# A 192-byte pad tile ahead of the FFN pool: four moving operands at another SBUF offset

## The chip, the cores and the metric

The kernel runs on one core of one Trainium2 chip. The metric is the device time of one execution in microseconds (us); the median of three executions of the kernel before is 2823.21 us.

## The reference

A decoder block on one sequence of 256 positions with 2048 channels, in float32. Two token mixers run on the same normalised input, their results are gated and merged, and a dense gated feed-forward network (FFN) follows. What matters for this change is the FFN:

```
def swiglu(h, w_gate_up, w_down):
    gate, up = jnp.split(h @ w_gate_up, 2, axis=-1)
    return (jax.nn.silu(gate) * up) @ w_down
...
x = x + gate_m[:, None, :] * mix                        # the mixers' half, ending with a projection w_o
h = modulate(rms_norm(x, norm_ffn_w[layer]), shift_f, scale_f)
x = x + gate_f[:, None, :] * swiglu(h, w_gate_up[layer], w_down[layer])
return rms_norm(x, final_norm_w)
```

The hidden width of the FFN is 5632, 44 tiles of 128.

## The kernel before

**Tiling.** Activations lie transposed: 128 channels on the partitions, 256 positions along the free dimension. A weight block is 128 x 1024 floats (512 KB): eight 128 x 128 tiles. Every weight of the block is read once, in such blocks.

**A block's way.** `load_next` (L131 to L147) issues the block's DMA into a ring of five `raw` tiles, ScalarE rounds it to `hi` (L144, type float32r), VectorE subtracts to get `lo` (L146). Up to four blocks are taken in ahead. For each 128 x 128 tile TensorE then runs three matmuls (L214 to L216 in `lin_items`; L237 to L239, the same, in `quad_items`; L1111 to L1113 for the last of the state-space mixer):

```
T_.matmul(ps[:, t, :], hi[:, s], h_, start=kt == 0, stop=False)
T_.matmul(ps[:, t, :], hi[:, s], al[:, kt, :], start=False, stop=False)
T_.matmul(ps[:, t, :], lo[:, s], h_, start=False, stop=kt == nk - 1)
```

The weights `hi`, `lo` are the stationary operand (one LDWEIGHTS each); the activations are the moving operand, 128 x 256, likewise split in a high and a low part. 24 such matmuls make a block. Below, three in a row, high-high, high-low, low-high, are called a triple.

**Order.** The code fixes every engine's order (`tc.manual_schedule()`); `pump()` emits one block's matmuls, then a step of the running mixer, then work on finished products. There is no planner. Stages in order of time: the adaLN scales and first products, eight units of the delta-rule mixer, eight of the state-space mixer, the merge, the projection `w_o` (32 blocks), the FFN's `w_gu` (176 blocks: 12 by `quad_items`, 164 by `lin_items`), the FFN's `w_dn` (88 blocks), the final norm.

**Where the moving operands lie.** Tiles of a pool follow one another in SBUF, and a pool opens where the last open one ends. The addresses of the built program, in bytes of each partition:

| tile | pool | used in | first byte | remainder by 512 |
|---|---|---|---|---|
| `hh`, `hl` | ap | both mixers' input products | 106176, 122560 | 192 |
| `yh`, `yl` | gl | mixers' output products | 169664 to 181952 | 192 |
| `mh`, `ml` | gl, mp | `w_o` | 138944, 147136, 186048 | 192 |
| `h2h`, `h2l` | ff | `w_gu` | 82432, 98816 | 0 |
| `fh`, `fl` | ff | `w_dn` | 115200, 160256 | 0 |
| `hi`, `lo` (stationary) | wp | everywhere | 66048, 29184 and on in steps of 4096 | 0 |

A moving slice is 1024 bytes long and a stationary one 512, so the remainder is that of every slice. The `ff` pool opens (L1174) after the mixers' pools are closed and so begins where `ca`, a pool of the mixers' constants, had begun. Its tiles in order: `h2h`, `h2l`, `fh`, `fl` (L1175 to L1178), the rotating `fth`/`htmp`, and `gf`, `sq`, `rstd`, which VectorE and ScalarE alone use. Before the first FFN matmul, L1184 to L1187 build `h2h` and `h2l`, sixteen steps of VectorE, ScalarE, VectorE.

Of the kernel before, what the change touches and what calls it, by code (L numbers as in the profile page):

```python
# [10 lines left out]
F32 = mybir.dt.float32  # L11
# [8 lines left out]
P = 128  # L20
# [5 lines left out]
NG = 8  # L26
FT = 44
BLK = 8
# LA: weight blocks kept ready ahead of the matmuls; NRAW, NAR: rings of raw blocks and of ada rows
LA = 3  # L30
NRAW = 5
# blocks between two halves of ada rows, by phase
SIDE, SIDE2 = 2, 8
SIDE3 = 6
# gate pairs of the ssm branch that fill the first gdn unit
GS = 6
# blocks per generator step (gdn units, misc, ssm units)
RG = [1.0] * 7 + [0.8]
R_M = 1.2
Q3 = [0, 8, 1, 9, 2, 10, 3, 11, 4, 12, 5, 13, 6, 14, 7, 15]  # L40
# [4 lines left out]
NPER = 4  # L45
DG = [0] + [1] * 7
DS = 1
# pairs whose blocks go to the tensor engine whole, as float32, by quad of K tiles
WH = [(0, 1, 7, 13), (4, 6, 8, 9, 11, 13, 15), (5, 7, 9, 11, 13, 15), ()]
NAR = 5  # L50
NCA = 2
LZ = 2

VB_ADA = 0
VN_MIX = 96
# [16 lines left out]
@with_exitstack  # L72
def block_kernel(ctx: ExitStack, tc: tile.TileContext, xT, cvec, vec, dskip, consts,
                 w_ada, w_misc, w_g0, w_g, w_s, w_gz, w_sz, w_gate, w_gp, w_sp, w_o, w_gu, w_dn, out):
    # Every weight is streamed once in blocks of 8 tiles (add_item); a block is split exactly into hi + lo,
    # and three products carry it. pump() emits one block's matmuls, one step of the running mixer
    # (gdn_mix, ssm_mix: generators) and pending work on finished products.
    nc = tc.nc
    V, A, T_, G = nc.vector, nc.scalar, nc.tensor, nc.gpsimd
    ctx.enter_context(tc.manual_schedule())  # L80
# [27 lines left out]
    ada = const.tile([P, 96], F32, name="ada")  # L108
# [18 lines left out]
    items, ready, posts, side, gens = deque(), deque(), deque(), deque(), deque()  # L127
# [6 lines left out]
    def load_next():  # L134
        src, *rest, whole = items.popleft()
        if whole:
            raw = wp.tile([P, BLK * P], F32, tag="lo", name="whole")
            nc.sync.dma_start(raw, src)
            ready.append((*rest, raw, None))
            return  # L140
        raw = wp.tile([P, BLK * P], F32, tag="raw", name="raw", bufs=NRAW)
        nc.sync.dma_start(raw, src)
        hi = wp.tile([P, BLK * P], F32R, tag="hi", name="hi")
        A.copy(hi, raw)  # L144
        lo = wp.tile([P, BLK * P], F32R, tag="lo", name="lo")
        V.tensor_sub(lo, raw, hi.bitcast(F32))  # L146
        ready.append((*rest, hi, lo))  # L147

    def finish_posts():
        while posts:  # L150
            posts.popleft()()

    def pump():
        while items and len(ready) < LA + 1:
            load_next()
        did = False
        if ready and ready[0][2] <= st_["done"]:
            mm, post, need, sync, hi, lo = ready.popleft()
            if sync:
                finish_posts()  # L160
            mm(hi, lo)
            posts.extend(post)
            st_["mm"] += 1
            did = True
        st_["wait"] -= 1.0
        if st_["gen"] is None and gens and gens[0][1] <= st_["mm"]:
            finish_posts()
            st_["gen"] = gens.popleft()
            st_["wait"] = 0.0
        if st_["gen"] is not None and (st_["wait"] <= 0.0 or not did):  # L170
            try:
                st_["wait"] = max(st_["wait"], -0.99) + next(st_["gen"][0]) * st_["gen"][2]
            except StopIteration:
                st_["gen"] = None
                st_["done"] += 1
        if posts:
            posts.popleft()()
        while len(posts) > PQ:
            posts.popleft()()
        st_["pumped"] += 1  # L180
        if side and st_["side"] and st_["pumped"] % st_["side"] == 0:
            side.popleft()()
# [64 lines left out]
    def z_items(blocks, unit, extra=None):  # L247
        pss = {}

        def mk(b):  # L250
            def mm(hi, lo):
                if b == 0:
                    for c in range(2):
                        pss[c] = plin.tile([P, 512], F32, tag="lin", name="ps_z")
                for k2 in range(2):
                    kt = 2 * b + k2
                    s = slice(k2 * 512, k2 * 512 + 512)
                    for c in range(2):
                        cs = slice(c * P, c * P + P)
                        T_.matmul(pss[c], hh[:, kt, cs], hi[:, s], start=kt == 0, stop=False)  # L260
                        T_.matmul(pss[c], hh[:, kt, cs], lo[:, s], start=False, stop=False)  # L261
                        T_.matmul(pss[c], hl[:, kt, cs], hi[:, s], start=False, stop=kt == KT - 1)  # L262
            return mm

        def done(c):
            if c == 0:
                unit["zs"] = gl_.tile([P, 2, 512], F32, tag="zs", name="zs")
            zs = unit["zs"]
            th = gl_.tile([P, 512], F32, tag="th", name="zth", bufs=1)
            A.activation(th, pss[c], AF.Tanh, scale=0.5)  # L270
            V.scalar_tensor_tensor(zs[:, c, :], th, 1.0, pss[c], ADD, MUL)  # L271
        for b in range(8):
            ex = extra[len(extra) * b // 8:len(extra) * (b + 1) // 8] if extra else []
            add_item(blocks[b], mk(b), ([lambda: done(0), lambda: done(1)] if b == 7 else []) + ex)
# [52 lines left out]
    def ada_fin(j0, j1):  # L327
        V.tensor_tensor(ada[:, j0:j1], ada2[:, j0:j1, 0], ada2[:, j0:j1, 1], ADD)
        V.tensor_tensor(ada[:, j0:j1], ada[:, j0:j1], vs[:, VB_ADA + j0:VB_ADA + j1], ADD)
# [7 lines left out]
    with tc.tile_pool(name="st", bufs=1) as st:  # L337
        x1 = st.tile([P, KT, S], F32, name="x1")
        wsc = st.tile([P, 2 * KT], F32, name="wsc")
        per = {}  # L340
# [197 lines left out]
        unit = [{"qkv": qkv0[h]} for h in range(2)]  # L538
# [41 lines left out]
    def gate_items(js, extra=()):  # L580
        extra = deque(extra)
        for j in js:
            def fin(ps, j=j):
                th = gl_.tile([P, 2, S], F32, tag="th", name="gth", bufs=1)
                A.activation(th, ps, AF.Tanh, scale=0.5)
                A.dma_start(gsd[:, j], th)
            lin_items([w_gate[4 * j + b] for b in range(4)], hh, hl, KT, [fin])
            for b in range(3):
                if extra:
                    src, mm, post, *rest = items[-4 + b]  # L590
                    items[-4 + b] = (src, mm, [extra.popleft()], *rest)
# [425 lines left out]
    for hu in range(NHU):  # L1017
        gens.append((gdn_mix(hu, unit[hu]), mark + DG[hu], RG[hu]))
        if hu == 0:
            z_items(w_gz[1], unit[1], late[:LZ])  # L1020
            gate_items(range(0, GS), late[LZ:])
            mark = st_["added"]
# [149 lines left out]
    phase_a.close()  # L1172

    with tc.tile_pool(name="ff", bufs=1) as ff:  # L1174
        h2h = ff.tile([P, KT, S], F32R, name="h2h")  # L1175
        h2l = ff.tile([P, KT, S], F32R, name="h2l")
        fh = ff.tile([P, FT, S], F32R, name="fh")
        fl = ff.tile([P, FT, S], F32R, name="fl")  # L1178
        F_.update(h=h2h, l=h2l, fh=fh, fl=fl, ff=ff)
        tmps = {}  # L1180
        for t in range(KT + 1):
            if t < KT:
                tmps[t] = ff.tile([P, S], F32, tag="fth", name="htmp", bufs=2)
                V.scalar_tensor_tensor(tmps[t], x2[:, t, :], wsf[:, t:t + 1], rf, MUL, MUL)  # L1184
                A.activation(h2h[:, t, :], tmps[t], AF.Identity, bias=ada[:, 48 + t:49 + t])
            if t > 0:
                V.scalar_tensor_tensor(h2l[:, t - 1, :], tmps[t - 1], ada[:, 47 + t:48 + t],  # L1187
                                       h2h[:, t - 1, :].bitcast(F32), ADD, SUB)
        while items:
            pump()  # L1190
        while side:
            side.popleft()()
        gf = ff.tile([P, KT], F32, name="gf")
        for j in range(8):
            lin_items([w_dn[j, b] for b in range(11)], fh, fl, FT, res_post(j, gf, ff))
        ada_fin(80, 96)
        V.tensor_scalar(gf, ada[:, 80:96], 0.5, None, MUL)
        while len(items) > 20:
            pump()
        for t in (1, 4, 7):  # L1200
            A.activation(x2[:, t, :], x2[:, t, :], AF.Identity, scale=vcol(VN_FIN + t))
        A.activation(dum, ones[:, 0:1], AF.Sqrt)
        flush()
        r = rstd_T(ff, sq_finish())
        for t in range(KT):
            if t in (1, 4, 7):
                G.tensor_tensor(x2[:, t, :], x2[:, t, :], r, MUL)
            else:
                V.scalar_tensor_tensor(x2[:, t, :], x2[:, t, :], vcol(VN_FIN + t), r, MUL, MUL)
            if t % 2 == 1:  # L1210
                (nc.sync if t % 4 == 1 else nc.scalar).dma_start(out[:, t - 1:t + 1, :], x2[:, t - 1:t + 1, :])
# [101 lines left out]
```

## Time and profile before

| | |
|---|---|
| median of 3 runs (lowest, highest) | 2823.21 us (2820.71, 2824.39) |
| span of the profiled execution | 2823.4 us |
| TensorE matmul busy | 2715.6 us, 96% |
| LDWEIGHTS busy | 2592.2 us, 92% |
| VectorE, ScalarE busy | 1887.0 us (67%), 1372.5 us (49%) |
| DMA, mean over the span | 201 GB/s |

The FFN's matmuls run from 2039.5 to 2808 us, the `w_o` stage before them from 1945.9 to 2033 us. Three views are used. The view of one tile gives for each line and engine the count, the shortest, median and longest duration in ns, and the start of the first and the last one in us; the distance of the first and the last start, divided by the number of steps between them, is the spacing of the instructions. The table of stretches gives the length of each, then busy time and count of PE, PEld, DVE, ACT, POOL, then the granted TensorE clock (1.00 is 2.4 GHz, 0.5 is 1.2 GHz), the DMA share and GB/s. The view of waits gives who waited for whom, us in total, how often, and the longest. PE is the matmul, PEld the weight load. A matmul's duration in the trace overlaps its neighbours'; the spacing of the starts is what adds up to time.

### The profile page before, as it was taken

The numbers are of one execution on the slowest core, as the hardware profiler recorded it, in microseconds if no ns is written. First come the engines' busy times: TensorE is split into PE (matmuls) and PEld (weight loads), VectorE is DVE, ScalarE is ACT, GpSimd is POOL, SyncE is SP. The second block draws the span as 40 slices with busy tenths as digits, with TensorE's granted clock in tenths as the row PEclk, the third lists the DMA queues.
The fourth block names the chain that finished last, engine by engine and source line by source line (L and its number), as shares of the span: only waits on it lengthen the run. The fifth ranks groups of instructions, "written<-read, shape, count | busy, mean of one in ns | idle before, by whom it ended". The sixth has DMA issues, their size and how long they took to land.

```text
span 2823.4 us, 51762 instructions
## 1 busy us (share of the span) xinstructions
PE 2715.6 (96%) x20930; PEld 2592.2 (92%) x20930; DVE 1887.0 (67%) x2794; ACT 1372.5 (49%) x2250; POOL 291.1 (10%) x684
## 2 busy tenths in 40 slices
PE   6999999999999999999999999999999999999998
PEld 5998898989899898898999999999999999999998
DVE  7887757667676676757777777768665565554444
ACT  3336454645545454554665655564444444443342
POOL 0000312303021130200000000002100000000000
PEclk8999999999999999999999999999999999999999
DMA  8986746556464655645655555558556666655553
GB/s 328 337 303 193 224 162 217 165 182 194 160 220 145 213 170 180 205 141 174 210 179 194 194 179 194 179 181 290 194 201 214 213 209 214 214 185 186 181 182 124
DMA packets 183282, 566.89 MB, mean 201 GB/s; under 512 B 34753, under 2 KB 43777, under 8 KB 183041
## 3 DMA queue, kind: packets, MB, share of 16 engines
q1 hardware_dynamic: 154306, 552.56, 58.9%
q10 hardware_dynamic: 28736, 11.01, 1.5%
q8 instruction: 164, 2.69, 0.4%
q14 instruction: 76, 0.62, 0.1%
HBM read 552.49 MB, written 11.01 MB: 200 GB/s over the span
## 4 chain that ended last, share of the span: by engine, by line
PE 65%; issue 11%; DVE 10%; POOL 6%; ACT 4%; DMA 2%; SPq 0%; ACTq 0%; DVEq 0%; POOLq 0%
PE ps_lin L214 14%; PE ps_lin L216 14%; PE ps_lin L215 14%; DVE lo L146 3%; PE ps_z L260 3%; PE ps_z L262 3%; PE ps_z L261 3%; POOL tm L724 2%; DVE cacc L288 1%; POOL Gt L726 1%; ACT hi L144 1%; DVE araw L324 1%; PE td L775 1%; PE tw L767 1%; DMA araw<-in_w_ada 1%
## 5 line engine op out<-in xcount | busy, mean ns | idle before, releaser
L146 DVE TENSOR_TENSOR lo<-raw,hi 128x1024 fp32r<-128x1024 f32 x825 | 1010.4, 1234 | 585.6 <-ACT hi L144 578.6
L144 ACT CAST hi<-raw 128x1024 fp32r<-128x1024 f32 x825 | 857.9, 1047 | 514.8 <-PE ps_lin L215 328.4
L214 PE MATMUL ps_lin<-hh,hi 128*128 128x256 f32 x1792 | 508.3, 284 | 0.0
L216 PE MATMUL ps_lin<-hh,lo 128*128 128x256 f32 x1792 | 500.5, 279 | 7.8 <-DVE lo L146 7.8
L215 PE MATMUL ps_lin<-hl,hi 128*128 128x256 f32 x1792 | 499.9, 279 | 0.0
L214 PE MATMUL ps_lin<-h2h,hi 128*128 128x256 f32 x1312 | 371.3, 283 | 0.0
L215 PE MATMUL ps_lin<-h2l,hi 128*128 128x256 f32 x1312 | 371.3, 283 | 0.0
L216 PE MATMUL ps_lin<-h2h,lo 128*128 128x256 f32 x1312 | 371.3, 283 | 0.0
L216 PEld LDWEIGHTS ps_lin<-hh,lo 128*128 128x128 f32 x1792 | 339.3, 189 | 9.2 <-DVE lo L146 9.2
L215 PEld LDWEIGHTS ps_lin<-hl,hi 128*128 128x128 f32 x1792 | 340.1, 190 | 4.0 <-issue 2.6
L214 PEld LDWEIGHTS ps_lin<-hh,hi 128*128 128x128 f32 x1792 | 339.3, 189 | 3.8 <-issue 2.4
L214 PE MATMUL ps_lin<-yh,hi 128*128 128x256 f32 x896 | 261.2, 291 | 20.3 <-DVE accg L572 18.7
L215 PE MATMUL ps_lin<-yl,hi 128*128 128x256 f32 x896 | 253.8, 283 | 0.0
L216 PE MATMUL ps_lin<-yh,lo 128*128 128x256 f32 x896 | 253.6, 283 | 0.0
L214 PEld LDWEIGHTS ps_lin<-h2h,hi 128*128 128x128 f32 x1312 | 251.9, 192 | 0.0
L215 PEld LDWEIGHTS ps_lin<-h2l,hi 128*128 128x128 f32 x1312 | 251.9, 192 | 0.0
L216 PEld LDWEIGHTS ps_lin<-h2h,lo 128*128 128x128 f32 x1312 | 251.9, 192 | 0.0
L260 PE MATMUL ps_z<-hi,hh 128*128 128x512 f32 x512 | 208.8, 408 | 2.4 <-DVE zs L271 2.0
L261 PE MATMUL ps_z<-lo,hh 128*128 128x512 f32 x512 | 202.0, 394 | 1.6 <-DVE lo L146 1.6
L262 PE MATMUL ps_z<-hi,hl 128*128 128x512 f32 x512 | 202.7, 396 | 0.0
L214 PE MATMUL ps_lin<-fh,hi 128*128 128x256 f32 x704 | 199.2, 283 | 0.0
L215 PE MATMUL ps_lin<-fl,hi 128*128 128x256 f32 x704 | 199.2, 283 | 0.0
(322 smaller groups left out, 5288.0 us busy)
## 6 DMA issues: line engine op xcount, KB each, us to landing
raw<-in_w_gu SPq DMA_DIRECT2D x176, 512.0 KB, 4.3
raw<-in_w_g SPq DMA_DIRECT2D x143, 512.0 KB, 4.2
raw<-in_w_ada SPq DMA_DIRECT2D x128, 512.0 KB, 4.7
raw<-in_w_s SPq DMA_DIRECT2D x96, 512.0 KB, 4.2
raw<-in_w_dn SPq DMA_DIRECT2D x88, 512.0 KB, 3.6
araw<-in_w_ada SPq DMA_DIRECT2D x64, 512.0 KB, 7.7
raw<-in_w_gz SPq DMA_DIRECT2D x64, 512.0 KB, 4.3
raw<-in_w_gp SPq DMA_DIRECT2D x64, 512.0 KB, 4.1
```

Of the source, the lines that this page charges most:

```text
L144: A.copy(hi, raw)
L146: V.tensor_sub(lo, raw, hi.bitcast(F32))
L214: T_.matmul(ps[:, t, :], hi[:, s], h_, start=kt == 0, stop=False)
L215: T_.matmul(ps[:, t, :], hi[:, s], al[:, kt, :], start=False, stop=False)
L216: T_.matmul(ps[:, t, :], lo[:, s], h_, start=False, stop=kt == nk - 1)
L260: T_.matmul(pss[c], hh[:, kt, cs], hi[:, s], start=kt == 0, stop=False)
L261: T_.matmul(pss[c], hh[:, kt, cs], lo[:, s], start=False, stop=False)
L262: T_.matmul(pss[c], hl[:, kt, cs], hi[:, s], start=False, stop=kt == KT - 1)
L288: V.scalar_tensor_tensor(acc[:, t, j:], x[:, t, :S - j], vcol(cw + 4 * t + 3 - j), acc[:, t, j:], MUL, ADD)
L324: V.scalar_tensor_tensor(raw, raw, 0.5, cact[:, hs], MUL, MUL, accum_out=ada2[:, j, hf:hf + 1])
L724: G.tensor_tensor(t3, F3[:, j + 1:16, j:j + 1].broadcast_to([64, n, j]), G3[:, j:j + 1, 0:j].broadcast_to([64, n, j]), MUL)
L726: G.tensor_tensor(G3[:, j + 1:16, 0:j], G3[:, j + 1:16, 0:j], t3, ADD)
```

## The change

A tile of 48 floats, 192 bytes in each partition, is allocated first in the `ff` pool and never used. So all later tiles of that pool move up by 192 bytes: `h2h` to 82624, `h2l` to 99008, `fh` to 115392, `fl` to 160448, each with remainder 192 by 512; `fth`/`htmp`, `gf`, `sq` and `rstd` move by as much. The pool's end moves from 212544 to 212736, still below the tile `accs`, which begins at 212960. No instruction is added, removed or moved: on every engine the rows of the built program and what each waits for are the same, one for one. Comment lines of the source are left out in the kernel after, and its line numbers are 2 higher from L54 on and 3 higher from L1175 on.

```
+OFF = 48
...
     with tc.tile_pool(name="ff", bufs=1) as ff:
+        ff.tile([P, OFF], F32, name="off")
         h2h = ff.tile([P, KT, S], F32R, name="h2h")
         h2l = ff.tile([P, KT, S], F32R, name="h2l")
         fh = ff.tile([P, FT, S], F32R, name="fh")
```

## Rows read from the trace of the kernel before

**Rows 1.** The page, part 1: busy time, share of the span, instructions.

```profile
PE 2715.6 (96%) x20930; PEld 2592.2 (92%) x20930; DVE 1887.0 (67%) x2794; ACT 1372.5 (49%) x2250; POOL 291.1 (10%) x684
```

**Rows 2.** Chain that ended last, 2100 to 2800 us: share by line.

```profile
by line: PE ps_lin L216 33.3%; PE ps_lin L215 33.3%; PE ps_lin L214 33.3%
```

**Rows 3.** Waits of PE from 2030 us to the end: total, times, longest.

```profile
PE ps_lin L237 <- ACT h2h L1185: 3.5, 1, 3.5
PE ps_lin L237 <- ACT hi L144: 2.5, 1, 2.5
...
PE ps_lin L239 <- DVE lo L146: 0.8, 1, 0.8
```

**Rows 4.** Table of stretches: `w_o`, the FFN's start, `w_gu`.

```profile
1950.00:2030.00 80.00, 80.00 (x708) 80.00 (x707) 53.52 (x59) 37.08 (x40) 10.05 (x7) 1.00 0.75 249
2039.00:2059.00 20.00, 16.23 (x94) 14.99 (x95) 18.63 (x36) 11.74 (x20) 0.00 (x0) 0.77 0.14 41
2100.00:2500.00 400.00, 400.00 (x3336) 400.00 (x3335) 234.50 (x285) 169.78 (x209) 0.00 (x0) 1.00 0.64 212
```

**Rows 5.** Tiles `h2h` and `fh`: FFN matmuls and weight loads.

```profile
L214 PEld LDWEIGHTS ps_lin<-h2h,hi x1312: 192/192/192, 2082.3 to 2554.2; 128*128 128x128 f32 x188
L214 PE MATMUL ps_lin<-h2h,hi x1312: 283/283/283, 2082.4 to 2554.3; 128*128 128x256 f32 x188
...
L216 PE MATMUL ps_lin<-fh,lo x704: 281/283/283, 2554.9 to 2808.0; 128*128 128x256 f32 x176
```

**Rows 6.** Tile `mh`: matmuls and weight loads of `w_o`.

```profile
L214 PEld LDWEIGHTS ps_lin<-mh,hi x160: 187/188/188, 1978.5 to 2032.5; 128*128 128x128 f32 x160
...
L216 PE MATMUL ps_lin<-mh,lo x160: 276/276/282, 1978.8 to 2032.9; 128*128 128x256 f32 x160
...
L237 PE MATMUL ps_lin<-mh,hi x96: 276/276/276, 1945.9 to 1978.2; 128*128 128x256 f32 x96
```

**Rows 7.** Tile `hl`: windows 549.8 to 571, 66.4 to 80, 1635.4 to 1645.9.

```profile
L215 PE MATMUL ps_lin<-hl,hi x63: 276/276/279, 549.7 to 570.8; 128*128 128x256 f32 x63
...
L389 PE MATMUL ps_q<-hl,hi x39: 281/281/281, 66.4 to 79.8; 128*128 128x256 f32 x39
...
L215 PE MATMUL ps_lin<-hl,hi x30: 281/281/281, 1635.3 to 1645.6; 128*128 128x256 f32 x30
```

**Rows 8.** Tiles `hl` and `yl` over the whole run.

```profile
L215 PE MATMUL ps_lin<-hl,hi x1792: 276/276/416, 304.9 to 1902.2; 128*128 128x256 f32 x200
...
L215 PE MATMUL ps_lin<-yl,hi x896: 276/281/420, 490.2 to 1874.0; 128*128 128x256 f32 x180
```

**Rows 9.** Timeline of PE at three rises of the clock: start, us, instruction.

```profile
395.94 0.41 PE L215 MATMUL ps_lin<-hl,hi 128*128 128x256 f32 x1
396.15 0.31 PE L216 MATMUL ps_lin<-hh,lo 128*128 128x256 f32 x1
...
522.39 0.34 PE L214 MATMUL ps_lin<-yh,hi 128*128 128x256 f32 x1
...
2058.28 0.38 PE L238 MATMUL ps_lin<-h2l,hi 128*128 128x256 f32 x1
2058.50 0.28 PE L239 MATMUL ps_lin<-h2h,lo 128*128 128x256 f32 x1
```

**Rows 10.** Tiles `hl`, `yl` just after the first two of these rises.

```profile
L215 PE MATMUL ps_lin<-hl,hi x25: 276/276/276, 396.8 to 404.9; 128*128 128x256 f32 x25
...
L215 PE MATMUL ps_lin<-yl,hi x2: 281/281/281, 522.9 to 523.3; 128*128 128x256 f32 x2
```

**Rows 11.** Line L144, 2100 to 2500 us: what ScalarE's cast waited for.

```profile
L144 ACT CAST hi<-raw x139: 1042/1047/1057, 2099.8 to 2498.9; 128x1024 fp32r<-128x1024 f32 x139
...
  PE ps_lin L215: 127.8, 70
```

**Rows 12.** VectorE's subtraction into `hl` (remainder 192) and `fl` (0).

```profile
L365 DVE TENSOR_TENSOR hl<-x,hh x16: 418/419/426, 27.1 to 190.7; 128x256 fp32r<-128x256 f32 x16
...
L1152 DVE TENSOR_TENSOR fl<-fth,fh x44: 424/426/426, 2078.6 to 2556.7; 128x256 fp32r<-128x256 f32 x44
```

More of the change, by code (lines that the diff above doesn't have):

```diff
@@ L52 @@
 LZ = 2
+OFF = 48
 VB_ADA = 0
@@ L1174, in block_kernel @@
     with tc.tile_pool(name="ff", bufs=1) as ff:
+        ff.tile([P, OFF], F32, name="off")
         h2h = ff.tile([P, KT, S], F32R, name="h2h")
```

## The prediction

> **What bounds the kernel now.** First the page: the matmul row is busy 96% of the span and the weight load 92% [rows 1]. Matmuls are pipelined, so busy time alone proves nothing; the chain and the waits do. From 2100 to 2800 us the chain that ended last is TensorE alone, a third on each of the three lines of a triple [rows 2], and from 2030 us on TensorE waits for VectorE or ScalarE only at the FFN's front: 3.5 us for `h2h`, 2.5 and 0.8 us for a block's `hi` and `lo` [rows 3], all before 2058.5 us, where the last rise of the clock to full speed falls [rows 9]. So from 2058.5 to the last FFN matmul at 2808.0 us [rows 5], 749.5 us, the time is the number of matmuls times their spacing, and nothing else.
>
> **The spacing is where the FFN differs.** The rows by tile give it as the distance of first and last start. In `w_gu` 1312 triples take from 2082.4 to 2554.3 us: 471.9 us over 1311 steps of three, 120.0 ns a matmul, every single one 283 ns long and every weight load 192 ns [rows 5]. In `w_o`, with the same three lines of code, the same weight ring and the same shapes, 3 x (96 + 160) = 768 matmuls start from 1945.9 to 2032.9 us: 87.0 us over 767 steps, 113.4 ns, matmuls 276 ns long and weight loads 188 ns [rows 6]. The granted clock is 1.00 in both stretches [rows 4], so the clock isn't the difference. Nor is the traffic: in `w_o` the DMA share is higher (0.75 against 0.64), VectorE is busier (53.5 of 80 us against 234.5 of 400) [rows 4], and yet the matmuls are closer together. What is left in the program is the first byte of the moving operand: remainder 192 by 512 in `w_o`, 0 in the FFN.
>
> **A second look, at the mixers**, which also use remainder 192, keeps this from being simple. There the same tile `hl` runs at two steps. In one window 63 of its matmuls lie between 549.7 and 570.8 us: 62 x 3 steps in 21.1 us, 113.4 ns, duration 276. In two others 39 and 30 of them take 13.4 and 10.3 us, together 23.7 us over (38 + 29) x 3 = 201 steps, 117.9 ns, duration 281 [rows 7]. Over the whole run the median of `hl` is 276 ns and that of `yl` 281 ns [rows 8]: both steps are common, and 283 is the median of neither. I call them the fast (113.4), middle (117.9) and slow (120.0) step. In the streams that I followed, TensorE keeps the step with which it came out of an interruption until the next one; the rise of the clock is such a start. After the rise at 396.15 us [rows 9] 25 matmuls of `hl` are all at 276; after that at 522.39 us [rows 9] `yl` is at 281 [rows 10]. [...]
>
> **The change part by part.** The pad costs no instruction and no time: it is never written or read. It moves three kinds of things.
> 1. The moving operands of the FFN. The uninterrupted stream from 2058.5 to 2808.0 us holds 3 x (1312 + 704) = 6048 matmuls from 2082.4 us on [rows 5], and before those 23.9 us / 0.120 = 199: 6247. At the fast step each saves 120.0 - 113.4 = 6.6 ns, 41.2 us. At the middle step 2.1 ns, 13.1 us. At the slow step 0. The durations (283 to 276 and 281) say 7 and 2 ns and agree. Matmuls ahead of 2058.5 us save nothing, because there waits and the low clock (0.77 on the mean of 2039 to 2059 us [rows 4]) set the pace.
> 2. The operands of VectorE and ScalarE in that pool. The nearest pair is the subtraction into `hl` (192), 419 ns, and into `fl` (0), 426 ns [rows 12]; so between -7 and +7 ns for each. On the path stand only the sixteen steps that build `h2h`, two VectorE instructions each: 32 x 7 ns, 0.2 us either way. I take 0.
> 3. What TensorE's speed asks of the suppliers. At the fast step a block of 24 matmuls takes 2.72 us instead of 2.88. ScalarE's cast takes 1.05 us a block, and 70 of 139 casts in `w_gu` waited for TensorE to free a `hi` tile, 127.8 us in all [rows 11], so the supply runs ahead. VectorE would go from 0.59 to 0.62 busy and DMA from 0.64 to 0.68, both below the 0.67 and 0.75 that `w_o` bears at that very spacing [rows 4]. This is why I cost the faster TensorE at no new wait. If that cover failed, the price would be of the size of the front's waits, 0.8 to 2.5 us each [rows 3].
>
> **A rule that speaks against the change.** The rows show 113.4 and 120.0 ns under one clock [rows 4 to 6]. The Trainium skill, "TensorE: Matmul & The Clock Gate", Part 2, says that TensorE has two independent SBUF read ports, and that loading the next weights takes no read bandwidth from the running matmul. By that the place of an operand shouldn't matter and the change would be worth 0. The trace has no experiment on it, but both spacings lie above the page's back-to-back gap (256 columns: an estimate of 262 cycles, 109 ns, by its table), so something that it doesn't name is paid in each. A third stretch speaks the same way: weight loads themselves last 192 ns in the FFN and 188 in `w_o` [rows 5, 6].
>
> **The rivals.**
> - *Fast step (forecast).* 2823.4 - 41.2 = 2782.2 us of span; the profiled span stands 0.2 us above the median of the runs, so 2782.0. For it: the nearest stage in code and shape, `w_o`, runs so throughout, and `hl` does so in more than half of its matmuls [rows 6, 8].
> - *Middle step.* The stream comes out of the clock's rise as at 522.39 us and stays there: 2823.2 - 13.1 = 2810.1 us. For it: the median of `yl` [rows 8]. Against it: nothing but counts. As a stream holds its step, I don't expect much between the two, though executions may differ from one another.
> - *No change: the address isn't the cause.* The slow step could be one more of the steps that a start falls into, and the FFN fell into it by chance, or it belongs to the FFN in a way that I don't see: 2823 us. Against it: the three runs lie within 3.7 us of each other, while a chance between steps would scatter them by 41 us, and in the rows of remainder 192 no median is 283. That the pad doesn't do what it says I leave out: the addresses of the built program are moved.
> - *Slower: a step above 120 ns.* The same chance, with a step that the trace doesn't hold long. At 122 ns, as far above the slow step as the middle one is below it, 6247 x 2.0 = 12.5 us: 2835.7 us. It decides from 0.9 ns a matmul on, where 0.2% is reached. Against it: no stream at full clock in these rows is that slow.
>
> **How the numbers follow.** Fast step 0.52, middle step 0.37, no change 0.07, slower 0.03, and 0.01 for a mixture of steps, which would be a gain too. The first two hold 0.89, and leaving out either leaves too much, so the range covers both. Below the fast step there is room for the 7 ns of the durations (43.7 us, 2.5 us more) and for the front, where one low-clock stretch more or less moves the stream's start by 1 to 3 us: 2776. Above the middle step the same front: 2813. A measurement of this kernel can tell about 0.2%, 5.6 us, from no change. Faster by more than that: 0.52 + 0.37 + 0.01 = 0.90. Within it 0.07, slower 0.03.
>
> **What would show it right or wrong.** Right: the FFN's matmuls are 276 ns long and 113.4 ns apart over the whole stream, its weight loads 188 ns, the first full-speed matmul near 2058 us and the last near 2767 us, and the stages before 2033 us as they were. The middle step shows as 281 ns and 117.9 ns, with the last one near 2795 us. If the durations stay at 283 ns, the address was not the cause. If the durations fall to 276 and TensorE shows waits for `hi` or `lo` inside the FFN, the cover in point 3 was wrong. The forecast is also wrong where executions of the same kernel fall into two groups some 28 us apart and the median lands in the upper one.

## The result and the profile after

The changed kernel takes 2785.22 us, the median of four executions: 2782.75, 2783.04, 2787.39 and 2811.1 us. Beside the kernel before (2823.80 us, 2820.71 to 2825.79) the ratio is 0.9884, 95% interval 0.9851 to 0.9917. The forecast was 2782.0 us in a range of 2776 to 2813. Four more executions later lay between 2780.92 and 2783.97 us, ratio 0.9855, 0.984 to 0.987. So by their times seven of eight executions are at the forecast's fast step (two of the seven were traced, and both are), and one is where the rival with the middle step was put (2810.1 us).

The profiled execution has a span of 2781.3 us, 42.1 less than before. Its lines are numbered 2 or 3 higher. The page's first part; the chain that ended last from 2100 to 2700 us; the waits of TensorE from 2030 us on (us, times, longest):

```profile
PE 2673.4 (96%) x20930; PEld 2549.9 (92%) x20930; DVE 1885.3 (68%) x2794; ACT 1372.3 (49%) x2250; POOL 289.3 (10%) x684
```

```profile
by line: PE ps_lin L218 33.3%; PE ps_lin L216 33.3%; PE ps_lin L217 33.3%
```

```profile
PE ps_lin L239 <- ACT h2h L1188: 3.5, 1, 3.5
PE ps_lin L239 <- ACT hi L146: 3.3, 1, 3.3
PE ps_sq L309 <- ACT sq L1130: 1.7, 2, 0.8
PE ps_lin L241 <- DVE lo L148: 0.7, 1, 0.7
```

The busy shares are those of [rows 1]: TensorE was "96% busy" before and is so now, 42 us sooner. Busy share says nothing of the spacing. The chain is as in [rows 2], and the waits are those of [rows 3]; none was added. The two waits at L309, 1.7 us in all, belong to the norm ahead of the FFN and to the final one; the kernel before has them too, and the prediction's list left them out. The tiles `h2h` and `fh`, the answer to [rows 5] (count; shortest, median, longest ns; first and last start):

```profile
L216 PEld LDWEIGHTS ps_lin<-h2h,hi x1312: 187/188/188, 2080.5 to 2526.2; 128*128 128x128 f32 x188
L216 PE MATMUL ps_lin<-h2h,hi x1312: 276/276/276, 2080.6 to 2526.3; 128*128 128x256 f32 x188
```

```profile
L216 PE MATMUL ps_lin<-fh,hi x704: 276/276/276, 2526.7 to 2765.7; 128*128 128x256 f32 x176
...
L218 PE MATMUL ps_lin<-fh,lo x704: 276/276/282, 2526.9 to 2765.9; 128*128 128x256 f32 x176
```

1311 steps of three in 445.7 us: 113.3 ns a matmul, where 120.0 stood before; durations 276 for 283, weight loads 188 for 192, as in the `w_o` of [rows 6]. Where the 42.1 us came from, by starts of the two traces: 1.7 us ahead of the FFN (its first matmul at 2037.8 instead of 2039.5; those stages have their own small spread), 0.1 us in the 12 blocks of `quad_items`, 26.2 us in `w_gu` (471.9 less 445.7), 14.1 us in `w_dn` (from 2526.3 to 2765.9 against 2554.3 to 2808.0). The front gains almost nothing, although its full-speed part runs closer: it waited 3.3 us for a block's `hi` instead of 2.5, and the clock came back to full speed at 2059.3 instead of 2058.5 us, although the FFN had begun 1.7 us sooner.

### The profile page after: what moved, and what is told of

Same layout as the page of the kernel before. It is cut to its first block, busy times and chain, and to the rows that moved or that the text cites. A ratio compares the mean times of both kernels' runs of the same rounds, so it can differ in the third digit from the quotient of the medians.

```text
span 2781.3 us, 51762 instructions
## 1 busy us (share of the span) xinstructions
PE 2673.4 (96%) x20930; PEld 2549.9 (92%) x20930; DVE 1885.3 (68%) x2794; ACT 1372.3 (49%) x2250; POOL 289.3 (10%) x684
## 4 chain that ended last, share of the span: by engine, by line
PE 61%; issue 12%; DVE 11%; POOL 8%; ACT 5%; DMA 3%; SPq 0%; ACTq 0%; DVEq 0%; POOLq 0%
PE ps_lin L216 13%; PE ps_lin L217 13%; PE ps_lin L218 13%; DVE lo L148 4%; PE ps_z L262 3%; PE ps_z L264 2%; PE ps_z L263 2%; POOL tm L726 2%; POOL Gt L728 2%; DVE cacc L290 2%; DMA raw<-in_w_g 1%; ACT hi L146 1%; DVE araw L326 1%; DMA araw<-in_w_ada 1%; PE td L777 1%
## 5 line engine op out<-in xcount | busy, mean ns | idle before, releaser
L216 PE MATMUL ps_lin<-h2h,hi 128*128 128x256 f32 x1312 | 362.1, 276 | 0.0
L217 PE MATMUL ps_lin<-h2l,hi 128*128 128x256 f32 x1312 | 362.1, 276 | 0.0
L218 PE MATMUL ps_lin<-h2h,lo 128*128 128x256 f32 x1312 | 362.1, 276 | 0.0
L216 PEld LDWEIGHTS ps_lin<-h2h,hi 128*128 128x128 f32 x1312 | 246.3, 188 | 0.0
L217 PEld LDWEIGHTS ps_lin<-h2l,hi 128*128 128x128 f32 x1312 | 246.3, 188 | 0.0
L218 PEld LDWEIGHTS ps_lin<-h2h,lo 128*128 128x128 f32 x1312 | 246.3, 188 | 0.0
L218 PE MATMUL ps_lin<-fh,lo 128*128 128x256 f32 x704 | 194.3, 276 | 0.0
```

## The experiments

Four questions: is it the address, and whose; how far does the good place reach; is the step drawn by chance; can the mixers gain too. "Spacing" is (last start - first start) of `h2h` over 1311 x 3 steps. Places are given as first byte of the moving operands, by 512, less that of `hi` and `lo`.

**Weights moved along.** The kernel before, with the pad in the weight pool: the FFN's operands are at 192 as in the changed kernel, but so are the weights.

```
     wp = ctx.enter_context(tc.tile_pool(name="wp", bufs=LA + 1))
+    wp.tile([P, 48], F32, tag="off", name="off", bufs=1)
```

> Kernel before with a 192-byte pad at the head of the weight pool instead of the FFN pool: everything above it moves up, so the FFN's moving operands lie at remainder 192 as in the changed kernel, but the stationary tiles hi and lo lie at 192 too; the mixers' moving operands go from 192 to 384. Theory A (a moving operand at a multiple of 512 is slow, whatever the weights' address): FFN at 113.4 or 117.9 ns a matmul, 2782 or 2810 us. Theory B (slow is the same remainder of moving and stationary operand): FFN at 120.0 ns, 2823 us, mixers as before. Theory C (chance at the stream's start, no address): any step in any execution.

2823.65 us (10 executions, 2817.84 to 2829.13), ratio 1.0002, 0.9992 to 1.0011. In its trace `h2h`, then `mh` of `w_o` (moving operand at 384, weights at 192):

```profile
L215 PEld LDWEIGHTS ps_lin<-h2h,hi x1312: 192/192/192, 2074.9 to 2546.9; 128*128 128x128 f32 x188
L215 PE MATMUL ps_lin<-h2h,hi x1312: 283/283/283, 2075.0 to 2547.0; 128*128 128x256 f32 x188
```

```profile
L238 PE MATMUL ps_lin<-mh,hi x96: 276/276/276, 1940.1 to 1972.4; 128*128 128x256 f32 x96
```

The FFN is back at 120.0 ns (472.0 us over 3933 steps) with its operands at 192. Theory A falls, B stands: what counts is the place of the moving operand relative to the weights. C has little left, since ten executions lie within 11 us.

The weight pool holds `raw`, `hi` and `lo`, so this pad also moved the places where DMA, ScalarE and VectorE write. The trace of the kernel before shows that these writes are not the other party: from 2100 to 2500 us all 3334 steps from one matmul's start to the next take 120 ns, the 330 through which ScalarE and VectorE are both idle, the 400 through which both work, and the 349 in which no DMA packet is under way. What is left in the weight pool is TensorE's own reading of the weights.

**The pad in front of `w_dn` only**, in the kernel before.

```
         h2l = ff.tile([P, KT, S], F32R, name="h2l")
+        ff.tile([P, 48], F32, name="off")
         fh = ff.tile([P, FT, S], F32R, name="fh")
```

> The pad stands between h2l and fh: w_gu keeps remainder 0, w_dn gets 192. A and B: 4134 matmuls of w_gu stay at 120.0 ns, the 2112 of w_dn go to 113.4 or 117.9 ns without any break or clock change between the two: 2823 - 13.9 = 2809 us, or 2823 - 4.4 = 2819 us. C (the step is set at the clock's rise and kept, whatever the address): w_dn has the step of w_gu, 2823 us or 2782 us.

2807.04 us (5 executions: 2804.51 to 2808.73, and one of 2818.72), ratio 0.9953, 0.9935 to 0.9971. The profiled execution is the one of 2818.72:

```profile
L214 PE MATMUL ps_lin<-h2h,hi x1312: 280/283/287, 2080.6 to 2552.6; 128*128 128x256 f32 x188
```

```profile
L214 PE MATMUL ps_lin<-fh,hi x704: 281/281/287, 2552.9 to 2801.3; 128*128 128x256 f32 x176
```

`w_gu` stays at 120.0 ns (472.0 us; its durations cycle through 280 to 287 ns here, with the same mean), and `w_dn`, without a break between the two, goes to 117.8 (248.4 us over 703 x 3): the middle step, 2819 us by the expectation. The other four fit the fast step's 2809 us, 2 us below it on the median; none of them was traced. So the step changes within a stream when the address changes. The last form of "it is the draw at the clock's rise, not the address" is gone.

**Other pads.** `OFF` of the changed kernel is set to another number of floats, nothing else.

```
-OFF = 48
+OFF = 64        # 256 bytes; in the others 8, 16, 32, 40, 56
```

> The changed kernel with a pad of 256 bytes instead of 192. A and B, if only the equal remainder is slow: steps as with 192, 2782 or 2810 us. If the slow place repeats every 256 bytes: 120.0 ns, 2823 us. If the distance decides between the two steps, all executions at one of them.

2823.77 us (10 executions, 2818.22 to 2826.05), ratio 0.9997, 0.9988 to 1.0007; spacing 120.0 ns:

```profile
L216 PE MATMUL ps_lin<-h2h,hi x1312: 283/283/283, 2081.2 to 2553.1; 128*128 128x256 f32 x188
```

The pad does nothing. Neither "any pad helps" nor "only an exact multiple of 512 is bad" holds: 256 is as bad as 0.

> The changed kernel with a pad of 32 bytes, the smallest that the pool gives. If slow is only the exactly equal remainder: 2782 or 2810 us. If slow is a neighbourhood of it (the two operands read near the same place for a while): 120.0 ns, 2823 us, or a spacing between.

2802.85 us (10 executions from 2797.47 to 2824.2), ratio 0.9941, 0.9922 to 0.9961. The profiled one (2809.97 us) has 117.8 ns:

```profile
L216 PE MATMUL ps_lin<-h2h,hi x1312: 280/280/280, 2080.6 to 2543.8; 128*128 128x256 f32 x188
```

Here the times scatter by 27 us. What the executions at 2797 and 2824 us did has no trace; if all that the fastest gains on 2823.7 us falls to the 6247 matmuls, they stood about 115.8 ns apart (an estimate), which is none of the three steps. By the median, 32 is better than 0 and worse than 192.

> The changed kernel with a pad of 128 bytes, half way between two slow places (0 and 256). Theory D (what counts is how far moving and stationary operand stand apart by 256 bytes): no start leads to the middle step any more, every execution at 113.3 ns, 2782 us, spread as in the kernel before, about 8 us. Theory E (only 0 and 32 are special, the draw stays elsewhere): two groups as with 192, 2782 and 2810 us.

2815.41 us (10 executions, 2811.82 to 2826.7), ratio 0.9974, 0.9963 to 0.9984; spacing 118.7 ns (466.7 us):

```profile
L216 PE MATMUL ps_lin<-h2h,hi x1312: 279/281/285, 2083.2 to 2549.9; 128*128 128x256 f32 x188
```

Both theories fall. Half way between two bad places is not the best place but one of the worse, and the durations cycle through 279 to 285 ns instead of holding one value. Distance alone is not the rule.

> Pad of 224 bytes, 32 before the next multiple of 256. Distance alone has failed: 128 gave 118.7 ns, 192 gives 113.3 or 117.8. Theory F (the direction counts: a moving operand that stands a little short of the next multiple of 256 keeps clear): 113.3 ns in most executions, 2782 us. Theory G (192 is a place of its own): as 32 on the other side, 115.6 to 120.0 ns, 2797 to 2824 us.

2813.12 us (4 executions, 2808.98 to 2814.52), ratio 0.9958, 0.9943 to 0.9973; spacing 118.3 ns (465.4 us):

```profile
L216 PE MATMUL ps_lin<-h2h,hi x1312: 277/280/285, 2079.5 to 2544.9; 128*128 128x256 f32 x188
```

F falls, G stands.

> Pad of 160 bytes, between 128 (118.7 ns) and 192 (113.3 or 117.8 ns). F: better than 128, worse than or like 192: 113.3 to 118 ns, 2782 to 2815 us. G: like 128, 118.7 ns, 2815 us.

2807.45 us (4 executions, 2807.02 to 2808.52), ratio 0.9941, 0.9924 to 0.9958; spacing 117.3 ns (461.5 us):

```profile
L216 PE MATMUL ps_lin<-h2h,hi x1312: 277/280/282, 2080.8 to 2542.3; 128*128 128x256 f32 x188
```

Better than 128 and far from 192: the gain does not rise gently towards 192. The number lies in F's range, which was wide, and not at G's 118.7 ns; but F fell with 224, so neither theory holds for all places.

> Pad of 64 bytes, the mirror image of 192 about 0 and 256. F: like 32 and 128, at 115.6 to 120 ns, 2797 to 2824 us. If distance were all after all: like 192, 2782 or 2811 us.

2808.35 us (4 executions, 2807.01 to 2809.9), ratio 0.9944, 0.9929 to 0.9959; spacing 117.8 ns (463.2 us), in the range of F. The mirror image of 192 is no second good place; distance is out for good.

```profile
L216 PE MATMUL ps_lin<-h2h,hi x1312: 279/279/279, 2080.6 to 2543.8; 128*128 128x256 f32 x188
```

**The changed kernel again**, without an edit.

> The changed kernel once more, for the spread. The pad of 192 bytes lies 64 bytes from the next multiple of 256. If the stream draws the fast or the middle step once per execution and keeps it: two groups of times, near 2783 and near 2811 us, with nothing between beyond 5 us. If the step wanders within an execution: times all over 2783 to 2811 us.

2783.27 us (2780.92 to 2783.97). The one of 2780.92 us was traced:

```profile
L216 PE MATMUL ps_lin<-h2h,hi x1312: 276/276/276, 2078.4 to 2524.2; 128*128 128x256 f32 x188
```

By their times all four are at the fast step; with the first four, one execution in eight is 28 us above the rest and none lies between 2788 and 2811 us. That fits one step for the whole of an execution, as expected; the 28 us are 6247 x (117.8 - 113.3) ns. The execution at 2811.1 us itself was not profiled; that it held the middle step is inferred from its time.

**The mixers moved as well**, in the changed kernel.

```
-OFF = 48
+OFF = 32
...
+    ca.tile([P, 48], F32, name="off0")
     cst = ca.tile([P, 4, P], F32, name="cst")
```

> Pad of 128 bytes in the FFN pool, and a pad of 192 at the head of the mixers' constants, so that every moving operand of the mixers and of w_o goes from remainder 192 to 384, which is 128 by 256. D: the mixers' matmuls too are all at 113.3 ns; some 3400 of 9600 are now at 117.8, so 15 us are gained beside the FFN's 41, less what the mixers' other waits take back: 2767 to 2778 us. E: mixers as now, no gain beside the FFN's.

2840.05 us (2839.19 to 2850.47), ratio 1.0066, 1.0047 to 1.0085: slower than before. `mh` of `w_o`, its moving operand at 384 with the weights at 0:

```profile
L217 PE MATMUL ps_lin<-mh,hi x160: 279/281/285, 1999.0 to 2055.6; 128*128 128x256 f32 x160
...
L240 PE MATMUL ps_lin<-mh,hi x96: 279/281/285, 1964.8 to 1998.6; 128*128 128x256 f32 x96
```

The 159 triples of the first row take 56.6 us, 118.7 ns, the value of the FFN at 128 in the run above, down to the same 279/281/285. In the weights-moved kernel the same tile, at the same remainder 384 but with the weights at 192, ran at 276 ns. One address, two spacings: the relative place decides, and 384 acts as 128 does. All matmuls of `w_o` and the mixers' longer streams pay it (of the mixers' 75 streams of 25 and more matmuls in this trace none is below 118.6 ns, and some stand at 120.0): `w_o` ends 22.9 us later (2055.8 against the 2032.9 of [rows 6]), which the FFN's gain of some 8 us at 118.7 ns doesn't cover. Neither D nor E had this.

**High parts at 0, low parts at 192**, in the kernel before.

```
         h2h = ff.tile([P, KT, S], F32R, name="h2h")
-        h2l = ff.tile([P, KT, S], F32R, name="h2l")
         fh = ff.tile([P, FT, S], F32R, name="fh")
+        ff.tile([P, 48], F32, name="off")
+        h2l = ff.tile([P, KT, S], F32R, name="h2l")
         fl = ff.tile([P, FT, S], F32R, name="fl")
```

> Tiles of the FFN pool in another order: the high parts h2h and fh at remainder 0, the low parts h2l and fl at 192. Per triple one or two matmuls stand at equal remainders with the weights being loaded beside them. If each matmul pays for its own operand alone: two at 120.0 and one at 113.3 ns, mean 117.8 ns, 2809 us. If one bad member sets the whole stream: 120.0 ns, 2823 us. If one good member frees it: 113.3 ns, 2782 us.

2810.42 us (2810.31 to 2810.93), ratio 0.9953, 0.9938 to 0.9968; spacing 117.8 ns (463.2 us). The mean that the first reading asked for, but not by its mechanism:

```profile
L214 PE MATMUL ps_lin<-h2h,hi x1312: 274/281/283, 2080.9 to 2544.1; 128*128 128x256 f32 x188
...
L215 PE MATMUL ps_lin<-h2l,hi x1312: 279/280/286, 2081.0 to 2544.3; 128*128 128x256 f32 x188
```

If each matmul paid for its own operand, `h2h` would hold one duration and `h2l` a lower one. Both wander, over nine and seven ns. So a matmul's duration doesn't follow from its own operand's place alone; which neighbour acts on it remains open. That the mean is also that of the middle step may be chance.

**Sixteen bytes on.** In the changed kernel `hh` and `hl` of the mixers go from 192 to 208 (by 256), to see whether a place without a draw lies there. One small tile of the mixers (`nb`) gives up its second buffer for the room.

```
-    hh = ap_.tile([P, KT, S], F32R, name="hh")
-    hl = ap_.tile([P, KT, S], F32R, name="hl")
+    hh = ap_.tile([P, KT * S + 64], F32R, name="hh")[:, 4:4 + KT * S].rearrange("p (k s) -> p k s", s=S)
+    hl = ap_.tile([P, KT * S + 64], F32R, name="hl")[:, 4:4 + KT * S].rearrange("p (k s) -> p k s", s=S)
```

> The changed kernel (FFN at 192), and in the mixers hh and hl moved on by 16 bytes within larger tiles, to 208 and 464, both 208 by 256; yh, yl, mh, ml stay at 192. Looks for a place without a draw: hh and hl at 192 share their time between 113.3 and 117.8 ns. If the good place reaches from 192 towards 208: all of their streams at 113.3 ns, some 8 us less than the changed kernel, 2775 us. If 192 is the only good place, as 160 (117.3) and 224 (118.3) suggest: none of their streams at 113.3 any more, some 3200 matmuls 4 to 5 ns longer, 2793 to 2800 us. The FFN stays at 113.3 or 117.8 either way.

2794.93 us (2789.05 to 2798.86), ratio to the kernel before 0.9887, 0.9863 to 0.991, so some 12 us above the changed kernel's 2783. One stream of `hl`, then `h2h`:

```profile
L217 PE MATMUL ps_lin<-hl,hi x38: 278/282/288, 1893.5 to 1906.7; 128*128 128x256 f32 x38
```

```profile
L216 PE MATMUL ps_lin<-h2h,hi x1312: 276/276/276, 2094.2 to 2539.9; 128*128 128x256 f32 x188
```

13.2 us over 111 steps: 118.9 ns in the mixers, while the FFN at 192 stays at 113.3 (445.7 us). Of the 58 streams of `hh` and `hl` with 25 and more matmuls in this trace one stands at 116.7 ns and the others at 119.0 to 119.4; in the changed kernel's trace they stand at 113.3 to 113.5 or at 117.8. So the second reading was right. Nothing waited for `nb` in this trace. The good place is narrow: 16 bytes on, it is gone. No version tried beats the changed kernel.

**All places in one table** (FFN, profiled executions; times are medians):

| moving less stationary, bytes | spacing, ns | median, us |
|---|---|---|
| 0 (kernel before; also with both at 192) | 120.0 | 2823.2; 2823.7 |
| 32 | 117.8 in the trace, scattered | 2802.9 |
| 64 | 117.8 | 2808.4 |
| 128 | 118.7 | 2815.4 |
| 160 | 117.3 | 2807.5 |
| 192 | 113.3, once in eight about 117.8 | 2783 to 2785 |
| 224 | 118.3 | 2813.1 |
| 256 | 120.0 | 2823.8 |

## Why the prediction was right, point by point

- **What bounds.** Right. Behind its front the FFN is a stream of matmuls with nothing to wait for, before and after; the time is count times spacing.
- **The size of point 1.** Right. 113.4 ns was read from `w_o`, 113.3 came. The term was 41.2 us, and 40.3 came in the two `lin_items` parts; the 1.3 us of the 199 matmuls before them were taken back by a wait and the later rise of the clock, and 1.7 us came from stages that the change doesn't touch. That the sum, 42.1 us, comes so near 41.2 is partly luck: what was lost and what was found nearly cancel.
- **Point 2, VectorE and ScalarE.** The 0 was right, its bound was not what I took it for. The subtraction into `fl` still takes 426 ns at remainder 192, so the 7 ns of [rows 12] are not the address:

```profile
L1154 DVE TENSOR_TENSOR fl<-fth,fh x44: 424/426/427, 2077.1 to 2528.6; 128x256 fp32r<-128x256 f32 x44
```

- **Point 3, the suppliers.** Right. The stretch from 2100 to 2500 us, to be held against [rows 4] (length; busy time and count of PE, PEld, DVE, ACT, POOL; clock, DMA share, GB/s):

```profile
2100.00:2500.00 400.00, 400.00 (x3532) 400.00 (x3531) 246.87 (x300) 179.40 (x222) 0.00 (x0) 1.00 0.67 222
```

VectorE 0.62 and DMA 0.67 were forecast as 0.62 and 0.68. From the clock's last rise to the last FFN matmul TensorE waits for no block.
- **The draw between two steps.** The two groups some 28 us apart are there. The odds look too high: the middle step had 0.37, and by its time 1 of 8 executions shows it; eight are too few to refute 0.37, which gives one or none in about one case of seven. I took the share of both steps in the mixers for the odds of one start. The FFN's stream starts with a rise of the clock, of which I had read two, and most of the mixers' streams don't. What sets the step at a start is still open.
- **The reason given.** Half right, and this is the part to learn from. "Remainder by 512 of the moving operand" came from comparing two stages in which the weights never moved. Three parts of it were not tested by anything in the trace: whose address (it is relative to the weights'), what period (256, not 512), and that every place but 0 would do (of the eight places tried in the FFN, one gives 113.3). The prediction needed none of the three, since the change puts the FFN exactly where `w_o` already stood. Had the pad been 256 or 128 bytes, the same argument would have forecast 2782 us, and 2824 or 2815 would have come.
- **The rule against the change.** As the prediction read the Trainium skill's sentence ("TensorE: Matmul & The Clock Gate", Part 2) that loading the next weights takes no read bandwidth from the running matmul, the place of an operand shouldn't matter. It does here: with the two operands at equal places a matmul costs 6.7 ns more than 64 bytes before the next multiple of 256. Moving either operand shows that their relative place decides, and the even 120 ns shows that the other engines' writes don't. Whether the two reads share bandwidth, and in which part of the chip the time is lost, is not shown. That both spacings lie above 109 ns was no evidence either way: every matmul here has its own weight load (20930 of each [rows 1]), so no run shows a stream without one.
- **No change, slower.** The first is refuted by the weights-moved and the `w_dn`-only kernels. No step above 120.0 ns was seen in the FFN's spacing; slower came only from moving the mixers.

## What to carry to other kernels

Where a stage is a dense stream of matmuls, divide the distance between the first and the last start by the count, for each stage: where two stages of one shape under one clock don't agree, compare the addresses of both operands, not the busy shares. Copy the relative place of moving and stationary operand from the stage that runs well, and measure it, rather than choose a round number: here 192 was worth 1.2 to 1.5%, 256 nothing, and 128 in the FFN, the mixers and `w_o` together cost 0.7%. A pad early in a pool moves everything behind it, so a pad for one stage can spoil another.

## What the runs showed of the hardware

- The spacing of 128 x 256 matmuls with a weight load each, at the granted clock 1.00, depends on where the moving operand lies relative to the weights: 113.3 to 120.0 ns, repeating after 256 bytes as far as tried (0 and 256: 120.0; 128 and 384: 118.7).
- At 128, 160 and 224 the matmuls' durations cycle (279/281/285 at 128), and the mean holds over thousands of them. At 0, 32, 64, 192 and 256 those of one line hold one value (for the first line of the triple 283, 280, 279, 276, 283); but in the `w_dn`-only kernel `w_gu` cycles through 280 to 287 at 0, with the same mean of 120.0.
- The one good place found, 192, is narrow: 160 gives 117.3, 208 (in the mixers) 118.9, 224 gives 118.3 ns.
- At 32, 128 and 192 executions of one and the same kernel differ, by up to 27, 15 and 30 us; ten at 256 lie within 8 us.
